# One decoder layer: four tiles for the rows of x, and one chain for each head of the second attention block

## The chip, the cores and the metric

The kernel runs on one core of a Trainium2 chip. The metric is device time in microseconds (us) of one execution. Five engines work in parallel, each on its own list of instructions, in the order of that list: TensorE (PE, matrix products; its weight loads are listed as PEld), VectorE (DVE), ScalarE (ACT), GpSimd (POOL) and SyncE (SP), which only issues transfers here. Instructions of different engines are ordered by semaphores alone: an instruction waits until what it reads has been written and until what it overwrites has been read.

## The reference

One layer over 256 tokens (`S`) of width 2048 (`D`), all in float32. In short:

```python
h    = rmsnorm(x) * g_pre
proj = h @ w_in                       # [A.q | A.k | A.v | B.c_q | B.c_kv | B.k_rope]
# A: 8 heads x 128, rotary on 32 channels, three dilated windows merged (256 tokens: one masked softmax)
# B: 8 heads, low-rank latents: q = rmsnorm(c_q) @ w_uq, [k | v] = rmsnorm(c_kv) @ w_ukv, shared rotary key, causal
x    = x + rmsnorm(concat(A, B) @ w_out)
x    = x + rmsnorm(relu(rmsnorm(x) @ w_up) ** 2 @ w_down)      # width 8192 inside
```

The change touches two places: the sum of squares of x's rows for the first norm, and the softmax and value product of the eight heads of B.

## The kernel before, in words

**Products.** Every weight is loaded as a float32 tile of 128 x 1024 (`raw`, 512 KB, issued by SP at line 198), and split in two parts that TensorE multiplies at a higher rate: `hi` on ACT (line 314) and `lo` = raw - hi on DVE (line 315). A product is then three matmuls (hi by hi, lo by hi, hi by lo). A tile serves 12 matmuls of 128 x 512, whether for `acc_qk` (queries and keys of heads 0 to 3 of A, tiles 0 to 16), `acc_v` (tiles 17 to 24) or `acc_q` (queries of heads 4 to 7, tiles 25 to 32). There are five `raw` buffers and eight `hi`/`lo` pairs: `raw` 22 can be loaded once `lo` 17 is made, `hi` 22 once PE is done with tile 14. The activations are not scaled by the norm before the product; the row's factor `rstd_pre` is applied when the product is copied out of PSUM (line 696, ACT).

**The order.** The program is written by a planner in Python. A `Flow` holds a clock that advances by a fixed cost with every matmul, and chains: Python generators that `yield` how many planned us shall pass before their next step. When the clock passes a chain's time, its next instructions are appended to the lists of their engines. So the numbers in the `yield`s set where in each list an instruction stands, and nothing else; on the chip it runs when its turn and its semaphores allow.

**The first norm** (`prelude`, `square_of`). The rows of x, 2 x 128 of 2048 values, are loaded by SP in eight pieces of 128 x 512 (line 582), between the weight loads, and squared and summed on ACT in four instructions of 128 x 1024 (line 569). The pieces go through two tiles only, with the tags `q` and `k`: the third and fourth half row take the place of the first and second. DVE adds the partial sums (line 587), POOL raises them to -1/2 (line 506, `rstd_pre`).

**From the products to the scores of A.** ACT copies q and k out (line 696), DVE applies the rotation (lines 623 to 626, with the table `trig`, a sine on ACT at line 612 after a table load), and then both are transposed in two steps: out to DRAM and back with the axes exchanged (POOL, lines 707 and 711), and in blocks of 32 on DVE (line 714). `sc_a`, the scores of a head, are two matmuls that need both blocks of k.

**Softmax and value product** (`softmax_pv`, for both blocks). DVE adds the mask and takes the maximum (line 638), ACT takes the exponential (line 649), DVE divides (lines 652 and 654), POOL writes the result to DRAM (`keep`, line 657) and loads it back with exchanged axes into `s` (line 660), DVE transposes blocks of 32 (line 662), PE multiplies with the values (`o_a`, `o_b`), and ACT and DVE split the output into `mixT` (lines 314 and 315). `DA` and `DB` hold the planned pauses between the steps, `D_TRIP` those around the two transfers. Scores and outputs of all heads share two PSUM banks in turn (`at_bank`).

**The heads of B** (`heads_b`). Six chains, `N_WORK[1]`, run over the eight heads; the first two take a second head (6 and 7) when their first is done. A chain starts when the queries, keys and rotary parts of its head are made (`made`, `qr_chain`, `kr_chain`). `vB`, the values, are copied out of PSUM by ACT (line 874). Around these heads PE works on the key, query and value products of B (`acc_k`, `acc_q`, `acc_v`, weight tiles up to 86) and then on the output product (`acc_o`, from tile 87).

Of the kernel before, what the change touches and what calls it, by code (L numbers as in the profile page):

```python
# [26 lines left out]
P = 128  # L27
D = 2048
S = 256
NB = S // P  # L30
KD = D // P
HA = 8
HB = 8
# [12 lines left out]
CW = 1024  # L46
# [35 lines left out]

N_WARM = 8
B_ORDER = ("k0", "qr", "q0", "v0", "k1", "q1", "v1")
N_WORK = (4, 6)
D_TRIP = (1.0, 6.0, 8.0)
OUT_PIECES = ((0, 0, 512), (1, 0, 512), (2, 0, 512), (3, 0, 256), (3, 256, 256))


# [42 lines left out]
MM = 512 / 2400 + 0.0025  # L132
# [139 lines left out]
def layer(nc, tc, io):  # L272
    flow = Flow()
# [25 lines left out]
    def at_bank(name):  # L299
        return next_bank(6, 2, name)  # L300


    def mm(out, a, b, start, stop, cost=MM):
        nc.tensor.matmul(out, a, b, start=start, stop=stop)  # L304
        flow.spend(cost)
# [205 lines left out]
    pa = pool("pa", "right")  # L511
# [50 lines left out]
    ss0h = con.tile([P, NB, 2], F32, name="ss0h")  # L562
    rstd0 = []

    squared = []

    def square_of(half, b, pc):
        junk = pa.tile([P, 1024], BF16, tag="v", name=f"junk0_{b}{pc}")
        nc.scalar.activation(junk, half, AF.Square, accum_out=ss0h[:, b, pc:pc + 1])
        squared.append((b, pc))  # L570
        yield 0

    def prelude():
        yield D_X0
        nc.scalar.dma_start(out=gcol, in_=io["gains"])
        for b in range(NB):
            for pc in range(2):
                half = pa.tile([P, NB + 1, 512], F32, tag="qk"[pc], name=f"xh{b}{pc}")
                half = half.rearrange("p b n -> p (b n)")[:, :1024]
                for i in range(2):  # L580
                    c = slice(i * 512, (i + 1) * 512)
                    nc.sync.dma_start(out=half[:, c], in_=io["x"][b * P:(b + 1) * P, pc * 1024 + i * 512:][:, :512])
# [91 lines left out]
    def heads_a(qkv, half, hs, after, delay):  # L674
        while any(c in flow.chains for c in after):
            yield 0.5
        yield delay
        for h in hs:
            nm = f"a{half}{h}"
            qT, kT = [qkv[w][:, :2, h * P:(h + 1) * P] for w in "qk"]  # L680
            sc = at_bank(f"sc_{nm}")
            mm(sc[:, 0:128], qT[:, 0], kT[:, 0], True, True, MM)
            mm(sc[:, 128:384], qT[:, 1], kT, True, True, 2 * MM)
            yield DA[1]
            yield from softmax_pv(pa, DA, sc, bias_a, SCALE_A,
                                  [qkv["v"][:, b, h * 128:(h + 1) * 128] for b in range(NB)], half * 4 + h, nm)
            yield DA[6]
# [33 lines left out]
    for half in range(2):  # L721
        qkv = {}
        for nms in (("qk", "v") if not half else "qkv"):
            accs = [acc for _, _, acc in proj(xT, [ch_a[half, nms]], f"{nms}{half}",
                                              bank_of=at_bank if (half, nms) == (0, "v") else None)]
            for i, nm in enumerate(nms):
                if half and nm == "v":
                    flow.finish(*heads)
                if not half and nm != "v":
                    t = early.tile([P, NB + 1, 512], F32, name=f"{nm}_{half}")  # L730
                else:
                    t = pa.tile([P, NB + (nm != "v"), 512], F32, tag=nm, name=f"{nm}_{half}")
# [4 lines left out]
        heads = [flow.start(heads_a(qkv, half, (h,), evacs, 2.5 + h * D_PAIR), 2.0) for h in range(4)]  # L737


    early.release()  # L740
# [60 lines left out]
    pb.tile([P, 80], F32, name="pb_pad")  # L801
    q_chain = flow.start(latent(cq, 1, "q", lat), 2.0)
    kr_chain = flow.start(shared_key(), D_KR)

# [4 lines left out]
    made = set()  # L809
# [30 lines left out]
            nc.vector.tensor_copy(qrT[:, 2 * i:2 * i + 2, :], t.rearrange("p (j s) -> p j s", j=2))  # L840
            yield 1.0

    def heads_b(hs):
        for h in hs:
            while any(c in flow.chains for c in (qr_chain, kr_chain)):
                yield 0.5
            while not {f"k{h // 4}", f"q{h // 4}"} <= made:
                yield 0.5
            yield DB[0]
            sc = at_bank(f"sc_b{h}")  # L850
            for o, b in ((0, 0), (128, 1)):
                n = (b + 1) * P
                qs = slice(b * P, (b + 1) * P)
                mm(sc[:, o:o + n], qT[:, h, qs], kT[:, h, :n], True, False, (b + 1) * MM)
                mm(sc[:, o:o + n], qrT[:, h // 2, qs], krT[:, h % 2, :n], False, True, (b + 1) * MM)
            yield DB[1]
            yield from softmax_pv(pb, DB, sc, bias_b, by_query, [vB[:, b, h, :] for b in range(NB)], HA + h, f"b{h}",
                                  lambda: f"v{h // 4}" in made)
            made.add(h)

    workers = []
    for what, ch in ch_b:
        if what == "qr":
            flow.finish(q_chain)
        if what in ("qr", "v0", "v1"):
            if what == "qr":
                qr = lat.tile([P, NB, HB, RB], F32, tag="cq", name="qr")
            for _, b, acc in proj(latT["q" if what == "qr" else "kv"], [ch], what):
                if what == "qr":
                    out = qr[:, b].rearrange("p h d -> p (h d)")  # L870
                else:
                    i = 4 * int(what[1])
                    out = vB[:, b, i:i + 4, :].rearrange("p h d -> p (h d)")
                nc.scalar.activation(out, acc[0], AF.Copy)
# [12 lines left out]
    ssy = [con.tile([P, 4], F32, name=f"ssy{b}") for b in range(NB)]  # L887
# [573 lines left out]
```

## Time and profile before

| | |
|---|---|
| median of 3 runs | 1038.7 us (1036.48 to 1038.93) |
| the profiled execution | 1039.18 us, span 1037.4 us |
| mean granted clock of TensorE | 0.992 |
| PE busy | 1015.7 us (98%), 4678 matmul records |
| PEld busy | 845.6 us (82%) |
| DVE busy | 838.4 us (81%) |
| ACT busy | 624.7 us (60%) |
| POOL busy | 95.0 us (9%) |
| moved by DMA | 266.02 MB, 256 GB/s over the span |

Times in the rows are us from the first instruction's start; the span is the time from the first to the last instruction, and the execution's own time is 1.8 us longer. A row of the timeline gives the start, the duration, the engine, the line, the operation with its tiles (out<-in, without buffer numbers), how many instructions the row holds, and in brackets how long the engine stood idle before it and what ended that. The end of a matmul is modelled and lies beyond the start of the next, so the pace of PE is read from start to start. A row of the stretches gives for each engine the busy us and in brackets the instructions, then the granted clock of TensorE (1.00 is full), the share of the DMA engines that was busy, and GB/s. `SPq`, `ACTq` and `POOLq` issue transfers.

### The profile page before, as it was taken

To read this page: it belongs to the slowest core of one execution; us is meant where nothing else is said; L and a number is where in the kernel's file an instruction comes from. 1 tells how busy PE (TensorE), PEld (TensorE's weight loads), DVE (VectorE), ACT (ScalarE), POOL (GpSimd) and SP (SyncE) were. 2 spreads that over 40 slices of the span, in tenths; PEclk is the share of its full clock that TensorE was granted. 3 is DMA by queue.
4 is the path that set the end of the run, shared out by engine and by line. 5 is a ranking of instruction groups with operands and counts; after the bars stand their busy time and mean duration, and the time that the engine had idled before them with its cause. 6 is when DMAs were issued, how large, how long until landed. Compare 5 with 4: busy or idle time off the path is not lost.

```text
span 1037.4 us, 13278 instructions
## 1 busy us (share of the span) xinstructions
PE 1015.7 (98%) x4678; PEld 845.6 (82%) x4678; DVE 838.4 (81%) x1125; ACT 624.7 (60%) x822; POOL 95.0 (9%) x148
## 2 busy tenths in 40 slices
PE   9988999999999999999999999999999999999996
PEld 6866889889788878888888888888888888888885
DVE  6576656675647669999999999897999999897896
ACT  6565436565536467666776767666666665756571
POOL 0010211102101010000100100000101000211100
PEclk9989999999999999999999999999999999999998
DMA  8878757655558478877989887589989867988972
GB/s 278 280 241 287 257 155 231 235 171 186 195 199 277 155 271 290 268 238 264 283 257 305 268 267 253 192 268 323 361 261 388 294 235 242 327 305 294 315 260 81
DMA packets 108370, 266.02 MB, mean 256 GB/s; under 512 B 9488, under 2 KB 28432, under 8 KB 107664
## 3 DMA queue, kind: packets, MB, share of 16 engines
q1 hardware_dynamic: 65488, 177.24, 50.3%
q0 software_dynamic: 19440, 68.17, 20.1%
q10 hardware_dynamic: 23376, 19.78, 6.0%
q8 instruction: 36, 0.59, 0.2%
q14 instruction: 30, 0.25, 0.1%
HBM read 232.12 MB, written 33.03 MB: 256 GB/s over the span
## 4 chain that ended last, share of the span: by engine, by line
PE 83%; DMA 7%; DVE 4%; ACT 2%; issue 2%; SPq 0%; POOL 0%; DVEq 0%; POOLq 0%; ACTq 0%
PE acc_u L304 26%; PE y L304 22%; PE acc_o L304 8%; PE m L304 6%; PE md L304 5%; DMA raw<-in_w_in 4%; PE acc_k L304 3%; PE acc_v L304 3%; PE acc_q L304 3%; PE acc_ckv L304 2%; DVE lo L315 2%; PE acc_cq L304 2%; DMA u<-in_w_down 1%; PE sc_b L304 1%; ACT hi L314 1%
## 5 line engine op out<-in xcount | busy, mean ns | idle before, releaser
L315 DVE TENSOR_TENSOR lo<-raw,hi 128x1024 fp32r<-128x1024 f32 (+2 forms) x205 | 232.8, 1158 | 79.9 <-ACT hi L314 78.9
L314 ACT ACTIVATE hi<-raw 128x1024 fp32r<-128x1024 f32 (+2 forms) x205 | 201.9, 1003 | 94.1 <-DMA raw<-in_w_in 27.9
L304 PE MATMUL acc_u<-hi,hT_hi 128*128 128x512 f32 x386 | 150.7, 391 | 0.3 <-ACT hT_hi L314 0.3
L304 PE MATMUL acc_u<-hi,hT_lo 128*128 128x512 f32 x386 | 150.3, 389 | 0.5 <-DVE hT_lo L315 0.5
L304 PE MATMUL acc_u<-lo,hT_hi 128*128 128x512 f32 x386 | 150.2, 389 | 0.0
L304 PE MATMUL y<-lo,uhi 128*128 128x512 f32 x358 | 139.5, 390 | 0.5 <-DVE lo L315 0.3
L304 PE MATMUL y<-hi,ulo 128*128 128x512 f32 x358 | 139.3, 389 | 0.0
L304 PE MATMUL y<-hi,uhi 128*128 128x512 f32 x358 | 139.3, 389 | 0.0
L318 ACT ACTIVATE hi<-raw,gcol 128x1024 fp32r<-128x1024 f32 x86 | 97.3, 1149 | 33.8 <-DMA raw<-in_w_up 14.8
L319 DVE SCALAR_TENSOR_TENSOR lo<-raw,gcol,hi 128x1024 fp32r<-128x1024 f32 x86 | 106.6, 1273 | 9.3 <-ACT hi L318 9.3
L304 PEld LDWEIGHTS acc_u<-hi,hT_lo 128*128 128x128 f32 x386 | 72.5, 188 | 16.0 <-DVE hT_lo L315 0.9
L304 PEld LDWEIGHTS acc_u<-hi,hT_hi 128*128 128x128 f32 x386 | 72.5, 188 | 15.2 <-ACT hT_hi L314 0.5
L304 PEld LDWEIGHTS acc_u<-lo,hT_hi 128*128 128x128 f32 x386 | 72.5, 188 | 14.9
L304 PEld LDWEIGHTS y<-lo,uhi 128*128 128x128 f32 x358 | 67.2, 188 | 15.2 <-DVE lo L315 1.3
L304 PEld LDWEIGHTS y<-hi,uhi 128*128 128x128 f32 x358 | 67.2, 188 | 14.1
L304 PEld LDWEIGHTS y<-hi,ulo 128*128 128x128 f32 x358 | 67.2, 188 | 13.8
L315 DVE TENSOR_TENSOR lo<-st_down,hi 128x1024 fp32r<-128x1024 f32 x46 | 55.0, 1219 | 0.8 <-ACT hi L314 0.8
L314 ACT ACTIVATE hi<-st_down 128x1024 fp32r<-128x1024 f32 x46 | 47.8, 1049 | 4.7 <-DVE st_down L371 2.9
L304 PE MATMUL acc_o<-hi,mixT_hi 128*128 128x512 f32 x128 | 50.4, 394 | 0.0
L314 ACT ACTIVATE hi<-u 128x1024 fp32r<-128x1024 f32 (+1 forms) x33 | 32.2, 979 | 29.5 <-PE acc_u L304 10.0
L304 PE MATMUL md<-hi,s 128*128 128x512 f32 x138 | 49.9, 389 | 0.0
L304 PE MATMUL acc_o<-hi,mixT_lo 128*128 128x512 f32 x128 | 49.9, 390 | 0.0
(348 smaller groups left out, 2044.8 us busy)
## 6 DMA issues: line engine op xcount, KB each, us to landing
raw<-in_w_up SPq DMA_DIRECT2D x86, 512.0 KB, 4.8
raw<-in_w_down SPq DMA_DIRECT2D x82, 512.0 KB, 6.4
raw<-in_w_in SPq DMA_DIRECT2D x55, 512.0 KB, 5.5
ab<-in_w_up POOLq DMA_DIRECT2D x17, 1024.0 KB, 7.2
raw<-in_w_out SPq DMA_DIRECT2D x32, 512.0 KB, 5.1
ab_down<-in_w_down POOLq DMA_DIRECT2D x11, 1024.0 KB, 9.3
ulo<-ukeep POOLq DMA_DIRECT2D x20, 512.0 KB, 6.3
rkeep<-r ACTq DMA_DIRECT2D x28, 256.0 KB, 3.4
```

The costliest lines, as they stand in the source:

```text
L304: nc.tensor.matmul(out, a, b, start=start, stop=stop)
L314: nc.scalar.activation(hi, src, AF.Copy)
L315: nc.vector.tensor_tensor(out=lo, in0=src, in1=hi.bitcast(F32), op=OP.subtract)
L318: nc.scalar.activation(hi, src, AF.Copy, scale=g)
L319: nc.vector.scalar_tensor_tensor(out=lo, in0=src, scalar=g, in1=hi.bitcast(F32), op0=OP.mult, op1=OP.subtract)
```

## The change

Rows of x: the four half rows have a tile each (`xh0`, `xh0b`, `xh1`, `xh1b`; two of them are new allocations of 4 KB per partition). All eight pieces are issued first, at the same eight places of SP's list as before, and no piece overwrites a tile that ACT still reads. The four squares come after the last piece, 1.5 planned us apart, instead of each after its two pieces.

Heads of B: one chain per head, with a buffer of its own for `s`, `pT` and `st` (`N_WORK[1]` is 8). A head may start when the head before it has issued its scores and 3 planned us (`D_TURNS[1]`) have passed. In both blocks the pause between the load of `s` and its transposition is 7 planned us and no longer 8 (`D_TRIP[2]`). `D_TURNS[0]` is 3.5, as `D_PAIR` was, so the spacing of A's heads is as before.

```diff
-N_WORK = (4, 6)
-D_TRIP = (1.0, 6.0, 8.0)
+N_WORK = (4, 8)
+D_TRIP, D_TURNS = (1.0, 6.0, 7.0), (3.5, 3.0)
...
     def prelude():
         yield D_X0
         nc.scalar.dma_start(out=gcol, in_=io["gains"])
+        xh = [[pa.tile([P, NB + 1, 512], F32, tag="qk"[b], name=f"xh{b}").rearrange("p b n -> p (b n)")[:, :CW],
+               pa.tile([P, CW], F32, name=f"xh{b}b")] for b in range(NB)]
+        for pc in range(4):
+            for b in range(NB):
+                c = slice(pc % 2 * 512, pc % 2 * 512 + 512)
+                nc.sync.dma_start(out=xh[b][pc // 2][:, c], in_=io["x"][b * P:(b + 1) * P, pc * 512:pc * 512 + 512])
+                yield D_X
+        yield D_SS
         for b in range(NB):
             for pc in range(2):
-                half = pa.tile([P, NB + 1, 512], F32, tag="qk"[pc], name=f"xh{b}{pc}")
-                half = half.rearrange("p b n -> p (b n)")[:, :1024]
-                for i in range(2):
-                    c = slice(i * 512, (i + 1) * 512)
-                    nc.sync.dma_start(out=half[:, c], in_=io["x"][b * P:(b + 1) * P, pc * 1024 + i * 512:][:, :512])
-                    yield D_X
-                flow.start(square_of(half, b, pc), D_SS)
-        while len(squared) < 4:
-            yield 1.0
+                junk = pa.tile([P, 1024], BF16, tag="v", name=f"junk0_{b}{pc}")
+                nc.scalar.activation(junk, xh[b][pc], AF.Square, accum_out=ss0h[:, b, pc:pc + 1])
+                yield 1.5
...
-    def heads_b(hs):
-        for h in hs:
...
-            yield DB[0]
+    turn_b = [0]
+
+    def next_turn():
+        turn_b[0] += 1
+        yield 0
+
+    def head_b(h):
+        while not {f"k{h // 4}", f"q{h // 4}"} <= made or any(c in flow.chains for c in (qr_chain, kr_chain)):
+            yield 0.5
+        while turn_b[0] < h:
+            yield 0.5
         sc = at_bank(f"sc_b{h}")
...
+        flow.start(next_turn(), D_TURNS[1])
         yield DB[1]
...
-            workers = [flow.start(heads_b(range(w, HB, N_WORK[1])), w * D_PAIR) for w in range(N_WORK[1])]
+            workers = [flow.start(head_b(h), DB[0]) for h in range(HB)]
```

Three places show how the lists move. The first is ACT's list at the end of the first product: `hi21` to `hi24` are weight tiles, `junk0_..` the four squares, `q_0` and `k_0` the copies of queries and keys out of PSUM, `trig` the sine with its table load. Before:

```order
L569 ACTIVATE junk0_10_475,ss0h_125<-xh10_383 128x1024
L314 ACTIVATE hi21_495<-raw21_493 128x1024
L314 ACTIVATE hi22_519<-raw22_517 128x1024
L314 ACTIVATE hi23_541<-raw23_539 128x1024
L569 ACTIVATE junk0_11_548,ss0h_125<-xh11_442 128x1024
L696 ACTIVATE q_0_535<-acc_qk0_0_0_0_126,rstd_pre_555 128x512
L696 ACTIVATE q_0_535<-acc_qk0_0_1_0_128,rstd_pre_555 128x512
L696 ACTIVATE k_0_536<-acc_qk0_0_0_1_127,rstd_pre_555 128x512
L696 ACTIVATE k_0_536<-acc_qk0_0_1_1_129,rstd_pre_555 128x512
L612 ACT_TABLE_LOAD
L612 ACTIVATE trig_123<-ang_485 128x384
L314 ACTIVATE hi24_587<-raw24_585 128x1024
```

Now:

```order
L314 ACTIVATE hi23_535<-raw23_533 128x1024
L579 ACTIVATE junk0_00_542,ss0h_125<-xh0_261 128x1024
L606 ACT_TABLE_LOAD
L606 ACTIVATE trig_123<-ang_479 128x384
L579 ACTIVATE junk0_01_554,ss0h_125<-xh0b_262 128x1024
L314 ACTIVATE hi24_558<-raw24_556 128x1024
L579 ACTIVATE junk0_10_571,ss0h_125<-xh1_263 128x1024
L314 ACTIVATE hi25_578<-raw25_576 128x1024
L579 ACTIVATE junk0_11_588,ss0h_125<-xh1b_264 128x1024
L314 ACTIVATE hi26_598<-raw26_596 128x1024
L690 ACTIVATE q_0_529<-acc_qk0_0_0_0_126,rstd_pre_607 128x512
L690 ACTIVATE q_0_529<-acc_qk0_0_1_0_128,rstd_pre_607 128x512
```

The copies of q and k stand behind `hi26` and no longer behind `hi23`, the sine ahead of them and no longer behind, and all four squares in one place.

The second is PE's list at the first scores of A (`sc_a00`, head 0), within the product `acc_q1` of the queries of heads 4 to 7. Before:

```order
L304 MATMUL acc_q1_0_0_0_722<-hi28_667,xT_hi_82 128x512
L304 MATMUL acc_q1_0_0_0_722<-lo28_668,xT_hi_82 128x512
L304 MATMUL acc_q1_0_0_0_722<-hi28_667,xT_lo_83 128x512
L304 MATMUL sc_a00_791<-k_0_536,q_0_535 128x128
L304 MATMUL sc_a00_791<-k_0_536,q_0_535 128x256
```

Now:

```order
L304 MATMUL acc_q1_0_1_0_723<-hi30_703,xT_hi_82 128x512
L304 MATMUL acc_q1_0_1_0_723<-lo30_704,xT_hi_82 128x512
L304 MATMUL acc_q1_0_1_0_723<-hi30_703,xT_lo_83 128x512
L304 MATMUL sc_a00_836<-k_0_530,q_0_529 128x128
L304 MATMUL sc_a00_836<-k_0_530,q_0_529 128x256
```

39 matmuls of `acc_q1` stood ahead of these scores; now there are 72.

The third is DVE's list around the transposition for head 0 of B (`pT_b0`), with `lo..` of the weight tiles, the mask and maximum of later heads (`s_b..<-sc_b..`) and the second half of a head's output (`mixT_lo<-o_b..`). Before:

```order
L315 TENSOR_TENSOR lo94_2472<-raw94_2469,hi94_2471 128x1024
L662 STREAM_TRANSPOSE pT_b0_2210<-s_b0_2209 128x384
L662 STREAM_TRANSPOSE pT_b1_2216<-s_b1_2215 128x384
L662 STREAM_TRANSPOSE pT_b2_2222<-s_b2_2221 128x384
L315 TENSOR_TENSOR lo95_2497<-raw95_2494,hi95_2496 128x1024
L662 STREAM_TRANSPOSE pT_b3_2247<-s_b3_2246 128x384
L315 TENSOR_TENSOR mixT_lo_80<-o_b0_2513,mixT_hi_79 128x256
L315 TENSOR_TENSOR mixT_lo_80<-o_b1_2518,mixT_hi_79 128x256
L315 TENSOR_TENSOR mixT_lo_80<-o_b2_2523,mixT_hi_79 128x256
L315 TENSOR_TENSOR mixT_lo_80<-o_b3_2533,mixT_hi_79 128x256
L638 ISA s_b6_2545,st_b6_2547<-sc_b6_2528,cst_121 128x128
```

Now:

```order
L315 TENSOR_TENSOR lo93_2429<-raw93_2426,hi93_2428 128x1024
L656 STREAM_TRANSPOSE pT_b0_2188<-s_b0_2187 128x384
L632 ISA s_b5_2452,st_b5_2454<-sc_b5_2446,cst_121 128x128
...
L315 TENSOR_TENSOR mixT_lo_80<-o_b0_2461,mixT_hi_79 128x256
L646 RECIPROCAL st_b4_2393<-st_b4_2393 128x2
...
L315 TENSOR_TENSOR lo94_2472<-raw94_2469,hi94_2471 128x1024
L656 STREAM_TRANSPOSE pT_b1_2233<-s_b1_2232 128x384
L632 ISA s_b6_2494,st_b6_2496<-sc_b6_2489,cst_121 128x128
```

Four heads went through this place together; now each passes alone, with one weight tile between it and the next. On PE, `sc_b0`, `sc_b1` and `sc_b2` stood next to each other, and so did `o_b0`, `o_b1` and `o_b2`; now 12 to 30 matmuls of the running products lie between the scores of one head and those of the next, and between `o_b0` and `o_b1` there are 12 matmuls of `acc_o` and the scores of head 6. The number and kind of PE's instructions are the same.

More of the change, by code (lines that the diff above doesn't have):

```diff
@@ L563, in layer @@
     rstd0 = []
[L565 to L571, printed above, removed]
     def prelude():
@@ L736, in layer @@
         flow.finish(*heads)
-        heads = [flow.start(heads_a(qkv, half, (h,), evacs, 2.5 + h * D_PAIR), 2.0) for h in range(4)]
+        heads = [flow.start(heads_a(qkv, half, (h,), evacs, 2.5 + h * D_TURNS[0]), 2.0) for h in range(4)]
     early.release()
@@ L800, in layer @@
     latT["q"] = [pb.tile([P, 4, S], F32R, name=f"cqT_{w}") for w in ("hi", "lo")]
-    pb.tile([P, 80], F32, name="pb_pad")
+    pb.tile([P, 64], F32, name="pb_pad")
     q_chain = flow.start(latent(cq, 1, "q", lat), 2.0)
@@ L841, in query_ropes @@
             yield 1.0
-    def heads_b(hs):
-        for h in hs:
[L845 to L848, printed above, removed]
-            yield DB[0]
[L850 to L859, printed above, removed]
+    turn_b = [0]
[7 more added lines that the diff above has]
+            yield 0.5
+        sc = at_bank(f"sc_b{h}")
+        for o, b in ((0, 0), (128, 1)):
+            n = (b + 1) * P
+            qs = slice(b * P, (b + 1) * P)
+            mm(sc[:, o:o + n], qT[:, h, qs], kT[:, h, :n], True, False, (b + 1) * MM)
+            mm(sc[:, o:o + n], qrT[:, h // 2, qs], krT[:, h % 2, :n], False, True, (b + 1) * MM)
+        flow.start(next_turn(), D_TURNS[1])
+        yield DB[1]
+        yield from softmax_pv(pb, DB, sc, bias_b, by_query, [vB[:, b, h, :] for b in range(NB)], HA + h, f"b{h}",
+                              lambda: f"v{h // 4}" in made)
+        made.add(h)
     workers = []
```

## The prediction

> **What bounds the kernel now.** I read the page first:
>
> ```profile
> span 1037.4 us, 13278 instructions
> PE 1015.7 (98%) x4678; PEld 845.6 (82%) x4678; DVE 838.4 (81%) x1125; ACT 624.7 (60%) x822; POOL 95.0 (9%) x148
> ```
>
> PE is busy nearly all the time, and the change removes none of its instructions. So it can save only where PE waits or runs slowly. I looked for such places from the start to the output product, in PE's rows and then by stretches:
>
> ```profile
> core 0: us, PE busy (x) PEld busy (x) DVE busy (x) ACT busy (x) POOL busy (x), PEclk, DMA share, GB/s
> 68.60:78.90 10.30, 6.36 (x16) 4.55 (x15) 8.18 (x13) 6.67 (x8) 4.36 (x7) 0.68 0.55 164
> 78.90:87.40 8.50, 8.50 (x39) 6.93 (x37) 3.71 (x4) 4.43 (x6) 1.01 (x2) 0.98 1.04 393
> 87.40:95.90 8.50, 4.31 (x13) 3.10 (x12) 8.47 (x13) 5.02 (x7) 0.00 (x0) 0.82 0.72 243
> 258.70:274.40 15.70, 13.78 (x70) 11.59 (x68) 8.90 (x22) 8.40 (x19) 2.62 (x4) 1.00 0.64 204
> ```
>
> Three holes: 68.6 to 78.9 (16 matmuls where 8.5 us elsewhere hold 39, clock 0.68), 87.4 to 95.9 (13), and a smaller one near 270. All three are sites of the change. The first, in PE's timeline:
>
> ```profile
> 66.78 0.39 PE L304 MATMUL acc_v<-hi,xT_hi 128*128 128x512 f32 x1
> ...
> 68.59 0.39 PE L304 MATMUL acc_v<-hi,xT_lo 128*128 128x512 f32 x1
> 70.59 0.50 PE L304 MATMUL acc_v<-hi,xT_hi 128*128 128x512 f32 x1 [1.61 <-ACT hi L314]
> 73.42 0.80 PE L304 MATMUL acc_v<-lo,xT_hi 128*128 128x512 f32 x1 [2.33 <-DVE lo L315]
> ...
> 78.71 0.61 PE L304 MATMUL acc_q<-lo,xT_hi 128*128 128x512 f32 x1
> 79.13 0.42 PE L304 MATMUL acc_q<-hi,xT_lo 128*128 128x512 f32 x1
> ```
>
> From 66.78 to 68.59 lie eight steps, so the full pace is 0.226 us a matmul. From 68.59 to 79.13, 10.54 us, 15 start (the stretch's 16 include one begun before); at full pace 3.39 us. **Hole A costs 7.15 us**: 4.4 of waiting for tile 24, and 2.8 because the matmuls that follow start 0.43 apart.
>
> ```profile
> 87.38 0.39 PE L304 MATMUL acc_q<-hi,xT_lo 128*128 128x512 f32 x1
> 90.66 0.46 PE L304 MATMUL sc_a<-k,q 128*128 128x128 f32 x2 [2.90 <-DVE k L714]
> 92.41 0.86 PE L304 MATMUL sc_a<-k,q 128*128 128x256 f32 x2 [1.29 <-DVE k L714]
> ...
> 96.60 0.40 PE L304 MATMUL acc_q<-hi,xT_hi 128*128 128x512 f32 x1
> ```
>
> From 87.38 to 96.60, 9.22 us, there are ten full matmuls (2.26) and the scores (under 0.9 for four records at that pace; I take 0.65). **Hole B costs 6.3 us**, again a wait (for the transposed keys) and a slow stretch after it.
>
> ```profile
> 268.79 0.92 PE L304 MATMUL o_b<-pT_b,vB 128*128 128x256 f32 x4 [0.43 <-DVE mixT_lo L315]
> 273.15 0.49 PE L304 MATMUL sc_b<-kT,qT 128*128 128x128 f32 x2 [1.48 <-DVE st_b L638]
> ```
>
> The last stretch lacks 15.70 - 13.78 = 1.9 us of PE; since a modelled end (0.39) lies 0.16 beyond the next start, two gaps are really 0.3 longer. **Hole C costs 2.2 us**: heads that share two PSUM banks queue on each other.
>
> **Why A is there.** SP's waits and its timeline, then ACT's:
>
> ```profile
> SPq L582 <- ACT junk L569: 11.6, 2, 6.0
> ...
> 38.86 0.34 SPq L582 DMA_DIRECT2D xh<-in_x  x1
> 47.51 0.34 SPq L582 DMA_DIRECT2D xh<-in_x  x1
> ```
>
> ```profile
> 44.05 1.06 ACT L314 ACTIVATE hi<-raw 128x1024 fp32r<-128x1024 f32 x1 [4.26 <-DMA raw<-in_w_in]
> 52.34 1.06 ACT L314 ACTIVATE hi<-raw 128x1024 fp32r<-128x1024 f32 x1 [3.91 <-DMA raw<-in_w_in]
> ...
> 58.26 1.06 ACT L314 ACTIVATE hi<-raw 128x1024 fp32r<-128x1024 f32 x1 [0.29 <-DMA raw<-in_w_in]
> 59.62 1.06 ACT L314 ACTIVATE hi<-raw 128x1024 fp32r<-128x1024 f32 x1 [0.29 <-DMA raw<-in_w_in]
> 60.58 1.04 ACT L569 ACTIVATE junk<-xh 128x1024 bf16<-128x1024 f32 x1
> 65.33 1.27 ACT L696 ACTIVATE q<-acc_qk,rstd_pre 128x512 f32<-128x512 f32 x2 [3.62 <-POOL rstd_pre L506]
> 69.50 4.83 ACT L314 ACTIVATE hi<-raw 128x1024 fp32r<-128x1024 f32 x5
> ```
>
> SP stood 11.6 us before two loads of x whose tile ACT had not yet squared, with the weight loads queued behind it. ACT then idled 4.26 and 3.91 us for weights, and the lead over PE was gone when ACT had to wait for `rstd_pre`: between `hi23` (59.62) and `hi24` (69.50) it made no weight tile, and PE ran dry at 68.6.
>
> **The change, part by part.**
>
> *Four tiles for x.* The two SP waits go; the loads stay in place. ACT gets back up to 4.26 + 3.91 = 8.2 us, so `hi23` stands at 51.5 to 52.5 instead of 59.62 (the rest of the spread is the transfers' own rate: 58.26 to 59.62 in steps of about 1.35 us a tile, half of the 12 x 0.226 = 2.7 us that PE needs for one). Then, in the new list, come four squares (1.04 and a read-out, say 1.15 each: 4.6), table and sine (under 1.8: they and the copies of k fill 66.6 to 69.5), and `hi24` to `hi26` (3.2): `hi26` ends near 62.5, `lo26` at 63.8, and the factor 1.2 later, near 65, as late as before. But tiles 24 to 26 are made, and PE, which would have begun tile 24 at 68.8 and so began tile 17 at 68.8 - 7 x 2.72 = 49.8, needs tile 27 only at 49.8 + 10 x 2.72 = 77.0; ACT can make it at 67.6, after the copies. **A goes: -7.15.** The added order costs nothing as long as this lead of some 9 us covers it; without it the squares, table and sine in front of `hi24` would cost PE their 6 us.
>
> *B.* The scores stand 33 matmuls later on PE, at 49.8 + (96 + 72) x 0.226 = 87.8. The keys must be transposed by then:
>
> ```profile
> 71.52 1.70 POOL L707 DMA_DIRECT2D keepq<-q  x2 [6.22 <-ACT hi L314]
> 79.84 0.54 POOL L711 DMA_DIRECT2D k<-keepk  x1 [0.46 <-DMA keepk<-k]
> 87.37 1.22 DVE L315 TENSOR_TENSOR lo<-raw,hi 128x1024 fp32r<-128x1024 f32 x1 [1.15 <-ACT hi L314]
> 91.31 1.04 DVE L714 STREAM_TRANSPOSE k<-k 128x512 f32<-128x512 f32 x1
> k<-keepk POOLq DMA_DIRECT2D x4, 256.0 KB, 5.1
> ```
>
> (The last row is of the list of transfers: KB each, median us from issue to landing.) Before, the second load of k came in at about 79.84 + 0.54 + 5.1 = 85.5, and the transpositions stood behind a `lo` that waited for weights: a second price of A. Now the sine is ready ahead of the copies, so the rotation starts when q is copied (66.3), not after the sine at 69.6: 3.3 us sooner. k comes in near 82.2; one `lo` and two transpositions later, near 85.5, the scores are free, 2.3 us before PE asks. **B goes: -6.3.** Its bounds: nothing saved if the keys' trip grows by 6 us, all if it stays.
>
> *Heads of B.* The same matmuls stand apart instead of in groups; what a single change between `sc_b` and the products costs, no row shows apart from them; I take nothing and keep 1 us as the upper end. The transfers of POOL are as many as before. **C goes: -2.2**, since no four outputs now queue for two banks. What is new: each `o_b` waits for a transposition right behind one weight tile. For head 0, DVE's list has `lo93`, then the transposition; ACT's has the last `vB` copy, then `hi93`. From the end of `acc_v` PE has 12 matmuls and the scores of head 5 before `o_b0` (2.7 + 1.2 = 3.9 us), against copy, hi, lo and transposition:
>
> ```profile
> 257.56 0.60 ACT L874 ACTIVATE vB<-acc_v 128x512 f32<-128x512 f32 x1 [4.27 <-PE acc_v L304]
> 264.20 1.22 DVE L315 TENSOR_TENSOR lo<-raw,hi 128x1024 fp32r<-128x1024 f32 x1
> 265.34 1.49 DVE L662 STREAM_TRANSPOSE pT_b<-s_b 128x384 f32<-128x384 f32 x3
> ```
>
> 0.6 + 1.06 + 1.22 + 0.5 = 3.4, and a few hand-overs. The cover is 0.5 us at most; I charge **+0.5**, bounds 0 and 2. A late head pushes the next one's slot along, so the misses do not add up in full. `D_TRIP` of 7 moves the outputs of A's heads forward by about six matmuls (1.4 us); no PE row waits there now, so I take nothing, bounds 0 and 1.
>
> **Sum**: 1039.2 (this execution) - 7.15 - 6.3 - 2.2 + 0.5 = 1024.0; it lies 0.5 above the median of 1038.7, so the median after is **1023.5**.
>
> Beside this, the Trainium skill, "TensorE: Matmul & The Clock Gate", section "What's actually happening", says that the clock falls to half after an idle window of about 3.4 us and returns after a busy one. The trace agrees: 4.4 us of waiting in A and 4.2 in B are followed by steps of 0.43, the 1.48 us of C is not. By this rule a wait that stays, but under 3.4 us, would carry no slow tail.
>
> **The rivals.**
>
> *B stays.* The keys' trip runs beside more weight loads (78.90 to 87.40 already has a DMA share of 1.04) and is no shorter; for it speaks that the factor comes as late as before, against it the sine's 3.3 us and the 7.5 us that PE's list gives. 1023.5 + 6.3 = 1029.8.
>
> *A stays.* The weights do not come sooner, because the DMA engines and not SP set their arrival, or the squares eat the lead. Against: ACT's idle times end with loads that SP issued right after its wait. 1023.5 + 7.15 = 1030.7. With both left over, the change does not do what it says: about 1036.5, within the noise of 1038.7 (0.3% is 3.1 us, about what a measurement can tell).
>
> *Slower: the heads' round trip.* If the way from scores to transposition is longer than the slots allow, all eight `o_b` wait in turn. For it: head 0's scores and transposition lay 28 us apart before, and now there are about 25:
>
> ```profile
> 236.92 3.93 PE sc_b L304 x24
> keep_b<-pT_b POOLq DMA_DIRECT2D x8, 192.0 KB, 4.9
> s_b<-keep_b POOLq DMA_DIRECT2D x8, 192.0 KB, 3.8
> ```
>
> Against: before, four heads shared each step; the two transfers take 4.9 and 3.8 us, the rest of the 28 us was queueing. With w us per head the time is 1023 + 8 w; from w = 1.9 it is slower than before, and at 2.5 it is 1043.
>
> **How the numbers follow.** Forecast 0.70 (1021.5 to 1025.5), B stays 0.10, A stays 0.07, smaller waits of the heads (1026 to 1034) 0.06, no gain 0.03, slower 0.04. Faster by over 0.3%: 0.93; same 0.03; slower 0.04. The range reaches from the lowest sum (no charge, 1 us more from C and the scatter of the runs: 1021) to the rivals A and B: 1031.
>
> **What would show it.** SP has no wait on `junk`; ACT no idle of 4 us for weights between 40 and 53; PE's clock is full from 68 to 97 and its rows have no bracket at `acc_v` or the first `sc_a`; `k` is transposed before 87.8; the outputs `o_b` stand singly with waits under 0.5 us. Wrong would be a wait of PE for `DVE k` over 2 us, a stretch below clock 0.9 after 60, or brackets of over 1 us at several `o_b`.

## The result, and the profile after

| | before | after |
|---|---|---|
| median of four runs, us | 1038.45 (1036.48 to 1038.93) | 1023.43 (1022.25 to 1025.14) |
| profiled execution, us | 1039.18 | 1022.25 |
| its span, us | 1037.4 | 1020.5 |

The ratio is 0.986, with a 95% interval of 0.984 to 0.988: the change makes the kernel 1.4% faster, 15.0 us by the medians. The forecast was 1023.5 us. The two profiled executions lie 16.9 us apart; the three terms of the sum were 15.65 without the charge of 0.5.

The page after, its first line and the line of busy times:

```profile
span 1020.5 us, 13280 instructions
PE 1010.1 (99%) x4678; PEld 842.9 (83%) x4678; DVE 839.3 (82%) x1125; ACT 624.3 (61%) x822; POOL 94.0 (9%) x148
```

PE's instructions are the same 4678. Of the 16.9 us, 5.6 are busy time (1015.7 to 1010.1), largely steps that no longer run at half clock, and the rest is time between instructions. The same stretches as before, and one over the outputs of the second block's first heads (busy time and count by engine, PE's clock, DMA share, GB/s):

```profile
core 0: us, PE busy (x) PEld busy (x) DVE busy (x) ACT busy (x) POOL busy (x), PEclk, DMA share, GB/s
68.60:78.90 10.30, 10.30 (x47) 8.51 (x47) 6.51 (x7) 5.92 (x7) 3.83 (x7) 1.00 1.00 334
78.90:87.40 8.50, 8.50 (x39) 7.06 (x38) 7.35 (x8) 4.25 (x4) 0.00 (x0) 1.00 1.01 353
87.40:95.90 8.50, 8.50 (x42) 7.17 (x42) 4.70 (x13) 5.24 (x9) 0.00 (x0) 1.00 0.72 227
240.00:260.00 20.00, 20.00 (x101) 17.08 (x100) 13.44 (x44) 10.38 (x27) 5.21 (x9) 1.00 0.67 207
```

The first stretch now holds 47 matmuls where it held 16, the third 42 where it held 13, and the clock is 1.00 in all of them. What PE still waits for up to 375 us (total us, times, longest):

```profile
PE warm L527 <- DVE zero L524: 1.2, 1, 1.2
PE acc_u L304 <- DVE hT_lo L315: 0.5, 1, 0.5
```

Neither is at a place of the change. All three holes are gone, and no output `o_b` waits. ACT and DVE on the way there:

```profile
50.55 2.11 ACT L314 ACTIVATE hi<-raw 128x1024 fp32r<-128x1024 f32 x2 [0.61 <-DVE ang L596]
60.46 1.05 ACT L314 ACTIVATE hi<-raw 128x1024 fp32r<-128x1024 f32 x1
63.87 1.26 ACT L690 ACTIVATE q<-acc_qk,rstd_pre 128x512 f32<-128x512 f32 x2 [2.36 <-POOL rstd_pre L506]
66.16 3.91 ACT L314 ACTIVATE hi<-raw 128x1024 fp32r<-128x1024 f32 x4
```

```profile
65.16 0.42 DVE L617 TENSOR_TENSOR rp_q<-q,trig 128x256 f32<-128x256 f32 x1 [2.13 <-ACT q L690]
...
81.00 1.22 DVE L315 TENSOR_TENSOR lo<-raw,hi 128x1024 fp32r<-128x1024 f32 x1 [1.15 <-ACT hi L314]
82.14 1.11 DVE L708 STREAM_TRANSPOSE q<-q 128x512 f32<-128x512 f32 x1
83.10 1.07 DVE L708 STREAM_TRANSPOSE k<-k 128x512 f32<-128x512 f32 x1
84.02 1.20 DVE L315 TENSOR_TENSOR lo<-raw,hi 128x1024 fp32r<-128x1024 f32 x1
85.15 1.08 DVE L708 STREAM_TRANSPOSE q<-q 128x512 f32<-128x512 f32 x1
86.08 1.08 DVE L708 STREAM_TRANSPOSE k<-k 128x512 f32<-128x512 f32 x1
```

The two tiles made at 50.55 are `hi22` and `hi23`, finished at 52.66; before, `hi23` was finished at 60.68. ACT still waits for the factor (2.36 us before 63.87), but by then `hi26` is made (60.46 to 61.51), and PE, which begins tile 24 at 68.65, never notices. The second k is transposed at 87.16. PE asks for it here:

```profile
87.46 0.39 PE L304 MATMUL acc_q<-hi,xT_lo 128*128 128x512 f32 x1
87.69 0.82 PE L304 MATMUL sc_a<-k,q 128*128 128x128 f32 x4
```

The cover is 0.53 us. That is thin, and several of the experiments turn on it.

### The profile page after: what moved, and what is told of

Read it like the earlier page. It is cut to its first block, busy times and chain, and to the rows that moved or that the text cites. A ratio compares the mean times of both kernels' runs of the same rounds, so it can differ in the third digit from the quotient of the medians.

```text
span 1020.5 us, 13280 instructions
## 1 busy us (share of the span) xinstructions
PE 1010.1 (99%) x4678; PEld 842.9 (83%) x4678; DVE 839.3 (82%) x1125; ACT 624.3 (61%) x822; POOL 94.0 (9%) x148
## 4 chain that ended last, share of the span: by engine, by line
PE 97%; DVE 1%; issue 1%; ACT 0%; POOL 0%; DVEq 0%; POOLq 0%; ACTq 0%
PE acc_u L304 26%; PE y L304 25%; PE acc_o L304 8%; PE md L304 6%; PE m L304 6%; PE acc_v L304 5%; PE acc_qk L304 4%; PE acc_q L304 3%; PE acc_k L304 3%; PE acc_ckv L304 3%; PE acc_cq L304 2%; PE sc_b L304 1%; PE acc_qr L304 1%; PE y L1328 1%; PE sc_a L304 1%
## 5 line engine op out<-in xcount | busy, mean ns | idle before, releaser
L315 DVE TENSOR_TENSOR lo<-raw,hi 128x1024 fp32r<-128x1024 f32 (+2 forms) x205 | 233.1, 1157 | 67.6 <-ACT hi L314 66.3
```

The source lines that it names most:

```text
L315: nc.vector.tensor_tensor(out=lo, in0=src, in1=hi.bitcast(F32), op=OP.subtract)
```

## Experiments

Each kernel was timed in rounds against the kernel before, in three groups of four kernels, each group on one chip. The ratio is to the kernel before on the same chip, whose median was 1037.6, 1037.1 and 1037.0 us in the three groups; microseconds of different groups compare less well than ratios.

### The two halves of the change apart

Four tiles for x alone: the new `prelude` in the kernel before, nothing else.

```diff
 N_WORK = (4, 6)
 D_TRIP = (1.0, 6.0, 8.0)
...
+        xh = [[pa.tile([P, NB + 1, 512], F32, tag="qk"[b], name=f"xh{b}").rearrange("p b n -> p (b n)")[:, :CW],
+               pa.tile([P, CW], F32, name=f"xh{b}b")] for b in range(NB)]
...
+                nc.scalar.activation(junk, xh[b][pc], AF.Square, accum_out=ss0h[:, b, pc:pc + 1])
```

> Only the four tiles for x, with the squares behind hi23; the second block keeps its six chains with their old distances and the old D_TRIP. My theory: the holes A (7.15 us) and B (6.3 us) both come from SP's wait on junk and go with it, hole C (2.2 us) stays with its waits at o_b and sc_b. 1038.4 - 13.45 = 1025.0 us, no wait of PE between 10 and 110 us. Rival: the heads' part has a hand in A or B (they share D_TRIP, and the pools move); then less than 13 us is gained here. Rival: the whole gain is from these two places and C was no loss at all; then the time is that of the full change, 1023.4.

Measured: 1026.02 us against 1037.64, ratio 0.988 (0.986 to 0.990): 11.6 us less by the medians, 12.4 by the ratio. The four executions stand in two pairs, near 1024 and near 1028; the profiled one is of the slower pair, and 1.6 us of its time are two late waits in the last product (`y`), which this edit does not touch. PE's waits up to 375 us, those of 0.4 us and over but for the two that every kernel here has:

```profile
PE sc_b L304 <- DVE st_b L632: 1.5, 1, 1.5
...
PE o_b L304 <- DVE mixT_lo L315: 0.4, 1, 0.4
```

A and B are gone, the two waits of C stand. The term of 13.45 us lies inside the interval of 10 to 15 us.

The second block's part alone: eight chains with turns, eight buffers and `D_TRIP` of 7, with the old `prelude`.

```diff
-N_WORK = (4, 6)
-D_TRIP = (1.0, 6.0, 8.0)
+N_WORK = (4, 8)
+D_TRIP, D_TURNS = (1.0, 6.0, 7.0), (3.5, 3.0)
...
+        flow.start(next_turn(), D_TURNS[1])
```

> Only the second block's eight chains with turns, its eighth buffers and D_TRIP of 7; x goes through two tiles as before. My theory: C goes and nothing else, 1038.4 - 2.2 = 1036.2 us; the brackets of PE at acc_v (1.61, 2.33) and at sc_a (2.90) stand as before, SP still stands 11.6 us before the loads of x. Rival: C was no loss of its own (the work behind it takes the time back): 1038.4. The two kernels' gains add up to that of the full change, 15.0 us, if the places do not act on each other.

Measured: 1035.24 against 1037.64, ratio 0.9975 (0.9958 to 0.9992), 2.4 us by the medians and 0.8 to 4.4 by the interval. PE's longest waits there:

```profile
PE sc_a L304 <- DVE k L714: 4.2, 2, 2.9
PE acc_v L304 <- DVE lo L315: 2.3, 1, 2.3
PE acc_v L304 <- ACT hi L314: 1.8, 1, 1.8
...
```

A and B stand, C is gone. The two halves gain about 12 and 2.5 us, together about as much as the whole change. So nothing shows that the places act on each other, but the intervals (5 and 3.5 us wide) could hide 2 us of it.

### Was it SP's wait, or the place of the squares?

The change does two things to x: its pieces no longer share tiles, and the squares move behind `hi23`. This kernel does only the first. It is the kernel before with two more tiles, each square where it was.

```diff
-                half = pa.tile([P, NB + 1, 512], F32, tag="qk"[pc], name=f"xh{b}{pc}")
+                if pc:
+                    half = pa.tile([P, CW], F32, name=f"xh{b}b")
+                else:
+                    half = pa.tile([P, NB + 1, 512], F32, tag="qk"[b], name=f"xh{b}")
```

> Four tiles for x, but each square stands where it stood before, right behind the two loads of its piece (the first one behind hi14), and not all four behind hi23; the rest is as in the kernel before, six chains included. It tells SP's wait apart from the place of the squares. My theory: the wait was the cause; ACT has idle time for weights of 1 to 2 us several times before 50 us, in which the squares find room, so A and B go here too: 1025.0 us, equal to the run with four tiles alone within 0.5 us, rstd_pre some 5 us sooner than there. Rival: what mattered is that hi11 to hi23 no longer have squares among them; then up to 4.6 us of lead is lost and PE waits at tile 24 again: 1025.0 + 4.6 = 1029.6 us or up to A's 1032.

Measured: 1031.93 us, ratio 0.995 (0.993 to 0.996). That is 5.9 us over the kernel with late squares, and not within 0.5: my theory fell. But the rival was not right either, since PE does not wait at tile 24. PE's timeline, and DVE's last transposition of k:

```profile
85.92 0.64 PE L304 MATMUL sc_a<-k,q 128*128 128x128 f32 x2 [3.99 <-DVE k L717]
87.68 1.22 PE L304 MATMUL sc_a<-k,q 128*128 128x256 f32 x2 [1.11 <-DVE k L717]
```

```profile
86.56 1.07 DVE L717 STREAM_TRANSPOSE k<-k 128x512 f32<-128x512 f32 x1
```

A went, B stayed: PE lost 5.1 us at the keys and had ten slow steps after it. So SP's wait, the one thing that this kernel takes away, is the cause of A, and B needs something else. The end of the last transposition shows what: 92.35 before, 87.63 here, 87.16 after the change. With A gone the keys come about 5 us sooner in either kernel. But PE too is sooner by A, and asks at 81.8 here and at 87.7 after the change. The late squares let the first copies, and with them the scores, be written later in the program: in PE's list the first score stands at row 344 in the kernel before and in this one, and at row 377 after the change, 33 matmuls later.

### The scores alone moved

That reading can be tried: squares at the old place as in the last kernel, and only the scores of the first four heads put later (row 383, so 39 matmuls and not the 43 of the expectation).

```diff
-        heads = [flow.start(heads_a(qkv, half, (h,), evacs, 2.5 + h * D_PAIR), 2.0) for h in range(4)]
+        heads = [flow.start(heads_a(qkv, half, (h,), evacs, (2.5 if half else 10.5) + h * D_PAIR), 2.0) for h in range(4)]
```

> The kernel with four tiles and the squares at their old places (1031.9 us), with one thing more: the scores of the first block's first four heads stand 43 matmuls later in PE's list. There A was gone but B had stayed: the second k was transposed at 87.6 us, as in the changed kernel (87.2), but PE asked for it at 81.8, where the changed kernel asks at 87.7. My theory now: what removed B in the changed kernel is not that the keys come sooner but that the late squares put the scores some 33 matmuls later in the list; so with the scores late and the squares early B goes as well: about 8 us less PE time lost, 1024 to 1026 us, no wait at sc_a. Rival: the keys then come later too, because they hang on the same queue of work: 1032. Rival: the place of the squares costs by itself, elsewhere: between 1027 and 1031.

Measured: 1024.74 us, ratio 0.987 (0.985 to 0.989), 7.2 us less than with the scores at the old place, on another chip; the ratios lie 0.8% apart. PE at the first scores:

```profile
89.03 0.81 PE L304 MATMUL sc_a<-k,q 128*128 128x128 f32 x4
```

No wait: the second k was transposed at 86.06, 3.0 us ahead. So the place of the scores in PE's list removes B, with the squares early or late, once A is gone. What the change's late squares did for B, a larger distance at one line does as well.

### How thin is the cover, and what does a wait cost?

The changed kernel with the first scores 12 matmuls sooner (row 365):

```diff
-        heads = [flow.start(heads_a(qkv, half, (h,), evacs, 2.5 + h * D_TURNS[0]), 2.0) for h in range(4)]
+        heads = [flow.start(heads_a(qkv, half, (h,), evacs, (2.5 if half else 0.0) + h * D_TURNS[0]), 2.0 if half else 0.0) for h in range(4)]
```

> The full change, but the first scores of the first block stand 12 matmuls (2.7 us) sooner in PE's list. In the changed kernel they start at 87.69, 0.53 us after the last transposition of k has ended (87.16). My theory: the cover was 0.5 us, so PE now waits 2.0 to 2.5 us there, in one piece or with a short second one, and with no slow stretch after it, since the wait is short: 1023.4 + 2.3 = 1025.7. Rival: the transpositions move up with it (another order on DVE) and PE waits for nothing: 1023.4. Rival: the clock falls after this wait as well, and a tail of some 2 us comes on top: 1027.7.

Measured: 1027.12 us, ratio 0.989 (0.987 to 0.991). PE's timeline, then the stretches around the wait:

```profile
87.64 0.70 PE L304 MATMUL sc_a<-k,q 128*128 128x256 f32 x2 [2.06 <-DVE k L708]
```

```profile
85.30:87.70 2.40, 0.34 (x4) 0.15 (x2) 2.29 (x3) 2.09 (x2) 0.00 (x0) 1.00 1.01 337
87.70:89.10 1.40, 1.40 (x6) 1.18 (x7) 0.69 (x5) 1.29 (x2) 0.00 (x0) 1.00 0.75 285
89.10:92.50 3.40, 3.40 (x9) 2.62 (x8) 2.40 (x3) 0.99 (x4) 0.00 (x0) 0.50 0.29 54
92.50:94.00 1.50, 1.50 (x9) 1.31 (x8) 0.00 (x0) 1.06 (x1) 0.00 (x0) 0.99 1.00 347
```

The wait has the expected size, 2.06 us, but the second rival was right about what follows: PE works for 1.4 us at full clock, and then the clock is 0.50 for 3.4 us, in which eight steps take 0.43 us. They cost 8 x 0.2 = 1.6 us; with the wait that is 3.7. The median is 3.7 above that of the change, which was timed on another chip; by the ratios it is about 3.2.

The same with eight copies on DVE ahead of the first k, to make the wait longer:

```diff
         yield D_LOADED[half]
+        if nm == "k" and not half:
+            slow = early.tile([P, 512], F32, name="slow")
+            for _ in range(8):
+                nc.vector.tensor_copy(slow, t[:, 1, :])
```

> As the run with the scores 12 matmuls sooner, and DVE copies 128x512 eight times (into a tile that nobody reads) ahead of the two transpositions of the first k: extra work of about 8 x 0.5 = 4 us, whose only purpose is to make the wait at the first scores longer. It tells whether the slow steps after a hole belong to the length of the wait. My theory: the wait grows to about 6 us and is followed by steps of 0.43 for ten matmuls or so, as before in A and B (4.4 and 4.2 us of waiting): 1023.4 + 6 + 2.3 = 1031.7, PE's clock under 0.9 in that stretch. Rival: no tail, because the tail in A and B was the pace of the weight tiles, not the clock: 1029.4.

Measured: 1030.91 us, ratio 0.992 (0.990 to 0.995). The copies took 3.66 us, the wait became two of 2.29 and 2.39 us, and the clock:

```profile
85.10:90.30 5.20, 0.61 (x3) 0.30 (x2) 5.13 (x7) 2.79 (x3) 0.00 (x0) 1.00 0.43 119
90.30:93.70 3.40, 3.31 (x8) 2.65 (x9) 2.05 (x8) 0.99 (x4) 0.00 (x0) 0.50 0.34 130
93.70:95.00 1.30, 1.30 (x7) 1.05 (x6) 1.07 (x1) 0.00 (x0) 0.00 (x0) 1.00 0.30 38
```

Again one stretch of 3.4 us at half clock, no longer than after the wait of 2.06 us. The pace is the clock's and not that of the weight tiles, as the theory had it: the slow steps come with a granted clock of 0.50. The wait was 4.7 us and not 6: the copies took 3.66 us and not 4, and the first transposition began at 81.79, 0.8 us sooner than in the run before (82.60).

With the scores only 6 matmuls sooner:

```diff
-        heads = [flow.start(heads_a(qkv, half, (h,), evacs, 2.5 + h * D_TURNS[0]), 2.0) for h in range(4)]
+        heads = [flow.start(heads_a(qkv, half, (h,), evacs, (2.5 if half else 1.2) + h * D_TURNS[0]), 2.0 if not half else 2.0) for h in range(4)]
```

> The full change with the first scores 6 matmuls (1.4 us) sooner; with 12 PE waited 2.06 us and a stretch of 3.4 us at half clock followed, which began 1.5 us after the wait. My theory: PE waits 0.8 to 1.1 us and no slow stretch follows: 1023.4 + 1 = 1024.4, clock 1.00 from 85 to 95. Rival: any wait near 1 us is enough for the slow stretch: 1026.

Measured: 1024.40 us, ratio 0.988 (0.986 to 0.990). The number fits, but the profiled execution says nothing on the question: in it PE lost 1.1 us to a late weight tile near 11 us, so that it asked for the keys at 87.87 and had no wait there. It shows that the cover at the first scores depends on what PE loses ahead of it; whether a wait near 1 us is followed by a slow stretch is left open by this run.

### The heads' round trip and the two banks

The slower case of the prediction was a chain of head to head waits of w us, 8 w in all. Here the transposition stands about 6 us sooner, so that most of the cover of the two transfers is gone.

```diff
-        yield D_TRIP[2]
+        yield D_TRIP[2] if wk is pa else 1.0
```

> The full change, but in the second block the transposition is put 1.0 behind the load of the turned scores instead of 7.0: every transposition and output of these heads stands about 6 us (one weight tile) sooner in the lists. It takes away most of the cover of the heads' round trip, the slower case of the prediction. In the changed kernel s_b lands at 240.52, 246.16, 248.15 and 256.16, the transpositions of the first four heads start at 246.71, 251.26, 256.00 and 260.74: covers of 6.2, 5.1, 7.8 and 4.6 us. My theory: with 6 us less only the heads whose cover is under 6 wait, by at most 1.4 us, and a head that waits pushes the later ones along, so the misses do not add up: 1024 to 1025.5 us. Rival, the prediction's slower case with its 8 w: w of 1.4 at each head, 1023.4 + 11 = 1034.6. Rival: nothing at all, 1023.4, because PE's outputs have matmuls ahead of them that hide a late transposition.

Measured: 1026.22 us, ratio 0.989 (0.987 to 0.990), 2.8 above the change and 0.7 above the expected range. PE at the outputs:

```profile
258.02 0.89 PE L304 MATMUL o_b<-pT_b,vB 128*128 128x256 f32 x4 [1.35 <-DVE pT_b L656]
```

One head waits, the fourth, whose cover was the smallest (4.6 us), by the 1.4 us expected; two later ones lose 0.26 and 0.15 us. That is 1.8 us; the other 1.0 stands at no output. There is no chain of eight waits, and the 8 w of the slower case was too much by far.

The changed kernel with turns 0.1 apart:

```diff
-D_TRIP, D_TURNS = (1.0, 6.0, 7.0), (3.5, 3.0)
+D_TRIP, D_TURNS = (1.0, 6.0, 7.0), (3.5, 0.1)
```

> The full change, but the turns of the second block's heads are 0.1 apart, not 3.0: eight chains and eight buffers stay, the heads stand closer together again. It tells the spacing apart from the number of chains. My theory: hole C was heads queueing for two banks, so it comes back in part, with waits of PE at o_b or sc_b of 1 to 3 us in all: 1024.5 to 1026.5. Rival: the eight buffers and chains are what removed it: 1023.4.

Measured: 1025.75 us, ratio 0.988 (0.986 to 0.990); the one wait of PE in the block:

```profile
254.62 1.54 PE L304 MATMUL o_b<-pT_b,vB 128*128 128x256 f32 x8 [1.70 <-DVE pT_b L656]
```

The time is the one expected, the wait is not: it is for a transposition, not for a bank. What the six chains had to do with the banks was asked next: four tiles for x, and the old loop over heads with eight chains and eight buffers.

```diff
-N_WORK = (4, 6)
+N_WORK = (4, 8)
...
-    pb.tile([P, 80], F32, name="pb_pad")
+    pb.tile([P, 64], F32, name="pb_pad")
```

> Four tiles for x as in the change, and in the second block the old loop over heads, only with eight chains and eight buffers in place of six; the old starts (3.5 apart), no turns, the old D_TRIP. It asks what it was about six chains that made hole C. In the kernel before, the scores of heads 6 and 7 stand between the outputs of heads 2 and 3 in PE's list, since their chains first have to end heads 0 and 1; with eight chains they stand before all outputs. My theory after the run without turns: C was this mixing of scores and outputs in two banks, so here the 1.5 us wait at sc_b goes; the outputs o_b0 to o_b3 still follow each other and may queue for some 0.4 to 1 us. 1025.0 - 1.5 to 1025.0 - 2.2: 1022.8 to 1023.8. Rival: only turns take it away; the wait shows up at another sc_b or o_b: 1025 to 1026.

Measured: 1028.01 us, ratio 0.991 (0.989 to 0.993), 2.0 above the same with six chains on another chip, where 1.5 to 2.2 less were forecast from 1025.0. PE's timeline and the clock behind it:

```profile
258.99 1.98 PE L304 MATMUL o_b<-pT_b,vB 128*128 128x256 f32 x8 [1.86 <-DVE mixT_lo L315]
```

```profile
260.00:265.00 5.00, 5.00 (x17) 4.03 (x16) 2.37 (x4) 2.72 (x4) 0.54 (x1) 0.66 0.79 258
```

The scores no longer stand among the outputs, but four outputs follow each other into two banks, and the third waits until DVE has read the first (the bracket names `mixT_lo`); a slow stretch follows. So eight chains with the old starts do not remove the loss at the two banks: the place of the wait moves, and PE loses at least as much there as with six (waits of 1.5 and 0.4 us). That they are slower than six is not shown by the times, since the intervals of the two ratios overlap. The run with turns of 0.1 has eight chains too, no four outputs in a row in PE's list, and no wait for a bank, but one of 1.7 us for a transposition. Of the versions tried, only those with turns of 3.0 and the full `D_TRIP` lose nothing at the outputs.

### A version with more cover

The change with the squares at their old places and the scores at row 383:

```diff
-                nc.scalar.activation(junk, xh[b][pc], AF.Square, accum_out=ss0h[:, b, pc:pc + 1])
+                flow.start(square_of(half, b, pc), D_SS)
...
-        heads = [flow.start(heads_a(qkv, half, (h,), evacs, 2.5 + h * D_TURNS[0]), 2.0) for h in range(4)]
+        heads = [flow.start(heads_a(qkv, half, (h,), evacs, (2.5 if half else 10.5) + h * D_TURNS[0]), 2.0) for h in range(4)]
```

> The changed kernel with the squares at their old early places and the first four heads' scores 6 matmuls later than in the change. If the experiments are right, no wait of PE is left between 10 and 350 us, and the thin cover of 0.5 us at the first scores grows to 2 to 3 us. My theory: the same time as the change, 1022.5 to 1023.5, because PE there has nothing left to lose but its own work. Rival: the run with early squares and late scores (1024.7, still with hole C of 2.2 us) was intrinsically faster, and this gives 1022.5 or less.

and beside it the changed kernel again:

> The changed kernel once more, unchanged, on the chip of these three, so that they can be set against it directly. 1023.4 us, as measured before; a difference of more than 1.5 us would show the size of what the chip alone does.

Measured: 1024.08 (1021.87 to 1025.70) and 1023.21 (1022.16 to 1023.46), ratios 0.987 and 0.986 with intervals that overlap almost wholly. No difference can be told. In the profiled execution of the first, PE has no wait between 10 and 350 us, and the cover at the first scores is 3.1 us (transposed at 86.24, asked for at 89.35). It has one wait near the end, in the last product (`y`), which the change does not touch:

```profile
962.56 0.50 PE L304 MATMUL y<-lo,uhi 128*128 128x512 f32 x1 [2.18 <-DVE lo L315]
```

Waits of 1.2 to 2.2 us stand there in some of these kernels' profiles and not in others. They blur comparisons of 2 us and less. No version tried here beats the change.

The second profile of the changed kernel has less cover than the first. DVE ends the last transposition 0.44 us after PE has begun the scores:

```profile
87.68 1.08 DVE L708 STREAM_TRANSPOSE k<-k 128x512 f32<-128x512 f32 x1
```

```profile
88.32 1.20 PE L304 MATMUL sc_a<-k,q 128*128 128x128 f32 x4
89.17 0.58 PE L304 MATMUL acc_q<-hi,xT_hi 128*128 128x512 f32 x1
```

The four matmuls take 0.85 us to the next one's start, where they took 0.46 in the first profile (87.69 to 88.15). So in this execution PE did wait for the keys, for 0.4 us, and no slow stretch followed.

## Why the prediction was right, point by point

**A: right, in mechanism and size.** SP's list of waits has no row for `junk` any more. `hi23` was forecast to start at 51.5 to 52.5 and did so near 51.6; `hi26` was to end at 62.5, measured 61.51; the factor was to come "near 65, as late as before", measured 63.87 for the copy that needs it; `hi27` was to be possible at 67.6, and ACT began it at 66.16. PE has no wait for a weight tile. Even with the squares at their old places A goes, so of the two reasons SP's wait is the one that made it.

**B: right in the result, its reasons weighted wrongly.** The prediction gave two things for it: 33 matmuls more ahead of the scores, and keys that come in sooner, with a margin of 2.3 us. The place of the scores was calculated well (87.8 forecast, 87.69 measured). The rotation began 4.5 us sooner and not 3.3 (65.16). But the keys were transposed at 87.16 and not at 85.5. The second load of k was issued at 75.51 and so came in near 82, as forecast; it is DVE's part that the step undercounted. It took one `lo` and two transpositions, 3.3 us, from there; DVE's list has two `lo` and four transpositions from 81.00 to 87.16, 6.2 us. The first of the two `lo` waited 1.15 us for its `hi` besides, in a place where the step expected no such wait once A was gone. The margin was 0.5 and not 2.3 us in one profile, and in the other it was gone. That B went all the same was in part luck. The run with early squares shows what this means: there the keys come about as early, the scores stand at their old row, and B stays with 5.1 us of waiting. The sooner keys alone do not remove B; the moved scores are needed. Whether these would do with the keys as late as before was not tried. The rival "B stays" deserved more than its 0.10; it was nearer than its chance said.

**C: right.** 2.2 us forecast, 2.4 measured alone (0.8 to 4.4). "No four outputs queue for two banks" is the mechanism that the run with eight chains and the old starts shows from its other side: it lets them queue, and loses 1.86 us at the third. In the kernel before it was less an output (0.43 us) than the scores of a late head (1.48 us) that waited there.

**The charge at `o_b0`: not needed.** The transposition for head 0 and the output that needs it:

```profile
246.71 0.57 DVE L656 STREAM_TRANSPOSE pT_b<-s_b 128x384 f32<-128x384 f32 x1
```

```profile
247.86 0.81 PE L304 MATMUL o_b<-pT_b,vB 128*128 128x256 f32 x4
```

It ends at 247.28, 0.58 us ahead: a cover of 0.5 us was forecast "at most", and it held, so nothing of the 0.5 was paid. `D_TRIP` of 7 and the changes between scores and products cost nothing that a row shows.

**The rivals.** "A stays" and "no gain" fell with the result. The slower case, the heads' round trip, was tried by taking the cover away: it costs 1.35 us at one head and 0.4 at two more, not w at each of eight.

**The sum.** 15.65 us of holes less 0.5 of charge; the profiled executions lie 16.9 us apart, the medians 15.0. Some 1.3 us of the profile's difference was in no term: short waits of 0.8 us at `acc_qk`, 0.3 at `acc_u` and 0.3 at `y` stand in the profile before and not in this one after. They come and go from profile to profile, and with them some of the agreement to 0.1 us between forecast and median is luck.

**The side sentence on the clock was wrong.** It held that a wait under 3.4 us would carry no slow stretch, as the 1.48 us of C carried none. A wait of 2.06 us did. The rows before already spoke against it: the 4.4 us in A and the 4.2 in B, which the prediction took for agreement, are each two waits with a matmul or two between, and the longest single ones are 2.33 and 2.90 us. Nothing in the sum rested on it.

## What to carry to other kernels

SP's list stood still on the reuse of one buffer and held up every load behind it; the price showed some 20 us later (47.5 to 68.6) and on another engine. Look for such a stall in the issuing queue's own waits. When a stall ahead of a consumer is removed, the consumer too asks sooner, so a later stall on the same path does not go by itself: compare when the data is ready with when it will be asked for, both in the new order. Outputs that share two banks want to be spaced in the list; more chains alone only moved the wait here.

## What the runs showed of the hardware

A short wait can be followed by a stretch at half clock, and not at once. After 2.06 us of waiting PE ran 1.4 us at full clock, then 3.4 us at 0.50 (87.64 to 92.5 above); after 1.86 us of waiting at an output the clock fell in the same way near 260 (0.66 over the stretch of 5 us). After waits of 1.35, 1.48 and 1.70 us no slow stretch came. In the kernel before, the slow part of hole A, whose beginning lies inside the second of its waits, is twice as long:

```profile
68.60:72.30 3.70, 0.88 (x3) 0.19 (x1) 2.58 (x9) 3.69 (x5) 0.78 (x1) 1.00 0.00 0
72.30:79.10 6.80, 5.68 (x13) 4.51 (x14) 5.68 (x6) 3.08 (x4) 3.79 (x7) 0.50 0.87 261
```

6.8 us is two times 3.4, so the stretches seem to come in pieces of 3.4 us, each decided by how busy PE was in the piece before. In the first of these two pieces PE was busy for 2.28 of 3.4 us, and a second followed; after pieces that were busy almost throughout (3.31 to 3.40 us) the clock came back. That reading fits all these rows; no run here tested it by itself. The Trainium skill, "TensorE: Matmul & The Clock Gate", section "What's actually happening", speaks of free-running windows of 3.4 us, of which an idle one halves the clock. The length of the slow stretches agrees with it (3.4, 3.4 and 6.8 us). That the window has to be idle throughout does not: around the wait of 2.06 us, and around those of hole A, no 3.4 us are without matmuls.
